# Layer 0 of a two-layer mixture-of-experts trunk: all rows normalised on TensorE and stored plainly, and expert 0's rows made by one-hot products ahead of the overflow branch

## The chip, the core and the metric

One core of a Trainium2 chip runs the whole program. The metric is the device time of one execution in microseconds; the profile's span, which begins with the first recorded instruction, lies within it. Engines: TensorE (PE, with its weight loads as PEld), VectorE (DVE), ScalarE (ACT), GpSimd (POOL), and SyncE (SP), which issues most transfers.

## What is computed

A two-layer backbone over 256 latent and 256 context tokens of width 1024. Each layer has a mixer and then a mixture of 16 experts, of which each token takes two. In layer 0 latent and context tokens go through the experts together, 512 rows in all; in layer 1 only the 256 latent ones. The part that matters here, cut down:

```python
h = rms_norm(x, norm2_g[l]) * (1 + m[:, :, 4]) + m[:, :, 3]
hc = rms_norm(xc, norm2_g[l]) * (1 + mc[:, :, 4]) + mc[:, :, 3]
tokens = jnp.concatenate([h.reshape(-1, D), hc.reshape(-1, D)], axis=0)
...
e_logits = e_logits[jnp.arange(T), g_sel]
top_v, top_i = lax.top_k(e_logits, MOE_TOP_K)
gate = jnp.einsum('tk,tke->te', top_w, jax.nn.one_hot(expert_id, MOE_EXPERTS, dtype=F32))
for e in range(MOE_EXPERTS):
    hid = jax.nn.silu(t @ w1[e]) * (t @ w3[e])
    out = out + gate[:, e:e + 1] * (hid @ w2[e])
```

## The kernel before

The work is written in Python and put in order, engine by engine, by a scheduler; only where a block is wrapped in `in_order(PE)` does TensorE follow the written order. A branch (`tc.If`) ends what can be moved: what is written before it is issued before it or, if the scheduler puts it there, in the block after it. Memory on chip comes from arenas with hand-written `get` and `free`, and a stream of weight pieces of 1 MB each (`self.ws`) fills whatever blocks are given to it, through SyncE's queue (L161). Each piece is split for three-pass products into a rounded part (ScalarE, L339) and a remainder (VectorE or GpSimd, L342), and each product is three matmuls (L348 to L350).

The stages around the change, all in layer 0:

- `finish` ends the mixer. It leaves `H`, the scaled but not yet normalised rows of the latent tokens (`H[0]`) and of the context tokens (`H[1]`), four tiles of 128 rows and 1024 columns, and the router's logits. Ahead of that it fills the two context tiles of the HBM tensor `hd` with the shift row by broadcast (L1339).
- `moe` takes the rows' factors (`rs`), and brings `H` to normalised rows in `hd`. For the two latent tiles TensorE multiplies by a diagonal matrix of the factors (L1440) and adds the shift as a product with three bf16 rows (L1441); ScalarE copies the result over `H[0]` (L1442), and SyncE stores it (L1443). For the two context tiles ScalarE scales in place (L1436), and GpSimd's queue adds the tile to what lies in `hd` (L1437). Meanwhile VectorE picks groups and experts, TensorE counts each row's place within its expert (the rank matmuls, L1486 to L1489), and VectorE makes the ranks (L1501), the gates and the largest count, `mxi` (L1514).
- `experts_rows` has, for each expert, `rows(e)`: a one-hot of its ranks (L1526), eight small matmuls for row numbers and gates (L1562, L1564), the row numbers (L1567), and a gather of up to 128 rows from `hd` through GpSimd's queue (L1530). `take(e)` transposes the gathered rows (L1576), and casts and splits them (L1585, L1586). `first` and `second` are the expert's weight products, the first in two halves of 24 matmuls. The written order is `rows(0)`, `rows(1)`, the overflow branch, and then in TensorE's order `take(0)`, and for each expert e the first half of `first(e)`, `hidden(e - 1)`, `take(e + 1)`, `rows(e + 2)`, the second half, and `second(e - 1)`.
- `overflow` loads `mxi` into a register of every engine (L1857) and branches on it (L1863). Its body, for experts with more than 128 rows, is not entered in this execution.

Of the kernel before, what the change touches and what calls it, by code (L numbers as in the profile page):

```python
# [10 lines left out]
BF = mybir.dt.bfloat16  # L11
I32 = mybir.dt.int32
AF = mybir.ActivationFunctionType
OP = mybir.AluOpType
# [4 lines left out]
P = 128  # L19
D = 1024  # L20
# [232 lines left out]
class Trunk:  # L253
# [1052 lines left out]
    def finish(self, l, mix):  # L1306

        F, nc = self.F, self.nc
        ns = len(self.X)
        A2 = F.get(ns, D)  # L1310
        for s in range(ns):
            self.mod_row(A2[:, s], l, 4, s)

        rts, bR = F.get(ns, KC, 32), F.get(ns, 32)
        self.bR = bR
        for s in range(ns):
            nc.vector.tensor_tensor(rts[:, s], self.rt,
                                    self.a2[l][:, s].rearrange("p (k o) -> p k o", o=1).to_broadcast([P, KC, 32]), op=OP.mult)

        pr, pq = F.get(ns, KC, 32), F.get(ns, 32)  # L1320
        for s in range(ns):
            nc.gpsimd.tensor_tensor(pr[:, s], self.rt,
                                    self.sh[l][:, s].rearrange("p (k o) -> p k o", o=1).to_broadcast([P, KC, 32]), op=OP.mult)
            nc.vector.tensor_reduce(pq[:, s], pr[:, s].rearrange("p k c -> p c k"), AX.X, OP.add)
        ps = self.bank()
        nc.tensor.matmul(ps[:, 0:32 * ns], self.msk("ones"), pq.rearrange("p s c -> p (s c)"), start=True, stop=True)
        nc.scalar.copy(bR, ps[:, 0:32 * ns].rearrange("p (s c) -> p s c", s=ns))
        F.free(pr, pq)
        self.ss, junk = F.get(4, 2), F.get(512, dt=BF)

        H = [F.get(2, D) for s in range(ns)]
        if ns == 2:
            self.hd = self.dp.tile([4 * P, D], F32, name=f"hd{l}")

            self.S3 = F.get(D, dt=BF)
            nc.scalar.dma_start(self.S3[0:3], self.mb2[0].rearrange("i h c -> i (h c)"))
            src = self.md[l, 1][1, :, 1].rearrange("(o h) c -> o h c", o=1)
            for t in range(2, 4):
                nc.scalar.dma_start(self.hd[t * P:(t + 1) * P, :].rearrange("p (h c) -> p h c", h=2),  # L1339
                                    src.to_broadcast([P, 2, 512]))  # L1340
        self.ws.add(F.fits(2048) - FA[l])

        lg, hfR = [self.bank("m"), self.bank("a")][0:ns], Ring(F, 2, 2, 256)
        wait = [], [], []

        def scaled(c, s):
            sl = slice(256 * c, 256 * c + 256)
            nc.vector.tensor_tensor(H[s][:, :, sl], self.X[s][:, :, sl],
                                    A2[:, s, sl].rearrange("p (o c) -> p o c", o=1).to_broadcast([P, 2, 256]), op=OP.mult)

        def logits(c, s):

            ps, hf = self.bank(), hfR()
            for kk in range(2):
                for i in range(2):
                    nc.tensor.transpose(ps[:, 256 * kk + i * P:256 * kk + (i + 1) * P],
                                        self.X[s][:, i, 256 * c + kk * P:256 * c + (kk + 1) * P], self.ident)
            nc.scalar.copy(hf, ps.rearrange("p (k t) -> p k t", k=2))
            for kk in range(2):
                k = 2 * c + kk  # L1360
                j = k % 4
                nc.tensor.matmul(lg[s][32 * j:32 * j + 32, 0:256], rts[:, s, k], hf[:, kk], start=(k < 4), stop=(k >= 4))

        def squares(c, s):
            if c % 2:
                for i in range(2):
                    t = 2 * s + i
                    nc.scalar.activation(junk, self.X[s][:, i, 256 * c - 256:256 * c + 256], AF.Square,
                                         accum_out=self.ss[:, t, c // 2:c // 2 + 1])

        def last(c, s):
            for i, f in enumerate((scaled, squares, logits)):
                wait[i].append((c, s))
                if len(wait[i]) > LAG[i] * ns:
                    f(*wait[i].pop(0))

        self.pool_share = 0
        run_all(self.out_half(l, 1, mix, ns, last))
        for i, f in enumerate((scaled, squares, logits)):
            for cs in wait[i]:  # L1380
                f(*cs)
        F.free(*self.gates, junk, hfR, rts, self.rt, A2)
        self.R.free(*mix)
        if ns == 2:
            self.xgR = Ring(F, 3, D)
            for x in self.xgR.bufs:
                nc.gpsimd.memset(x, 0.0)
        self.ws.add(max(0, F.fits(2048) - FB[l]))
        if l:
            self.swap()  # L1390
        for t in range(2 * ns):
            self.dbg(f"xm{l}_{t}", self.x(t))
        self.moe(l, H, lg)
# [17 lines left out]
    def moe(self, l, hd, lg):  # L1411

        nc, F = self.nc, self.F
# [13 lines left out]
            stt(L[:, t], lp[:, 32 * t:32 * t + 32], rs[:, t:t + 1], self.bR[:, t // 2], op0=OP.mult, op1=OP.add)  # L1427
        if ns == 2:


            H, hd, dgR = hd, self.hd, F.get(2, P)
            for t in range(2):
                nc.scalar.activation(dgR[:, t], self.ident, AF.Copy, scale=rs[:, t:t + 1])
            for t in range(2):
                h, g = H[0][:, t], H[1][:, t]
                nc.scalar.activation(g, g, AF.Copy, scale=rs[:, 2 + t:3 + t])  # L1436
                nc.gpsimd.dma_start(hd[(2 + t) * P:(3 + t) * P, :], g, accum_op=OP.add)  # L1437
                for c in range(2):
                    sl, ps = slice(512 * c, 512 * c + 512), self.bank("a")
                    nc.tensor.matmul(ps, dgR[:, t], h[:, sl], start=True, stop=False)  # L1440
                    nc.tensor.matmul(ps, self.oneb[0:3], self.S3[0:3, sl], start=False, stop=True)  # L1441
                    nc.scalar.copy(h[:, sl], ps)  # L1442
                nc.sync.dma_start(hd[t * P:(t + 1) * P, :], h)  # L1443
            F.free(*H, self.S3, dgR)
        tmp = []

        def T(n):
# [91 lines left out]
    def experts_rows(self, l, nt, hd, rk, G, VAL, mxi):  # L1539
# [16 lines left out]
        def rows(e):  # L1556

            oh = ohR()
            self.one_hot(oh, "iota", rk, e)
            tb = self.bank("m")  # L1560
            for t in range(nt):
                nc.tensor.matmul(tb[:, 0:2], oh[:, t], self.vi[:, t], start=(t == 0), stop=(t == nt - 1))  # L1562
            for t in range(nt):
                nc.tensor.matmul(tb[:, 2:5], oh[:, t], VAL[:, t, e], start=(t == 0), stop=(t == nt - 1))  # L1564
            ohs[e] = oh
            gt, dst, xg = gtR(), ddR(), xgR()
            nc.vector.tensor_scalar(dst, tb[:, 0:1], tb[:, 1:2], BIG, op0=OP.add, op1=OP.add)  # L1567
            self.gather(hd, xg, dst)
            nc.vector.tensor_reduce(gt, tb[:, 2:5], AX.X, OP.add)  # L1569
            st[e] = xg, gt, dst  # L1570

# [7 lines left out]
        def take(e):  # L1579

            xh, xl = xs[e] = xhR(), xlR()
            for b in range(2):
                ps = turn(b, st[e][0])
                pv = ps.rearrange("p (k t) -> p k t", k=4)
                nc.scalar.copy(xh[:, 4 * b:4 * b + 4], pv)  # L1585
                nc.vector.tensor_tensor(xl[:, 4 * b:4 * b + 4], pv, xh[:, 4 * b:4 * b + 4].bitcast(F32),  # L1586
                                        op=OP.subtract)

        def first(e):

# [72 lines left out]
        yy = {}  # L1663
        rows(0)
        rows(1)
        self.overflow(l, nt, P, (rk, G), mxi, xt, put, uR.bufs[0], yR.bufs[0])
        self.ws.add(F.fits(2048))
        self.ws.keep(2, self.end[l])
        with self.in_order(PE):
            take(0)  # L1670
            for e in range(NE + 1):
                f = first(e) if e < NE else iter(())
                next(f, None)
                if e == NE - NP:
                    self.pool_share = 0

                if e:
                    hidden(e - 1)
                if e + 1 < NE:
                    take(e + 1)  # L1680
                if e + 2 < NE:
                    rows(e + 2)
                next(f, None)
                if e:
                    second(e - 1)
                if e == NE - NP:
                    F.free(yR)
                    G2 = [F.get(D) for s in range(2)]
                    for s in range(2):
                        self.mod_row(G2[s], l, 5, s)  # L1690
                    for t in range(nt):
                        back(t, xgR.bufs[1 + t] if t < 2 else None)
        self.pool_share = 2
        F.free(ohR, gtR, ddR, uR)
        if self.early:
# [378 lines left out]
```

## Time and profile before

| what | value |
|---|---|
| three runs | 1195.66, 1200.86, 1201.46 us; median 1200.86 |
| profiled execution | 1201.99 us |
| its span | 1200.2 us |
| TensorE busy | 1084.5 us (90%) |
| VectorE busy | 785.6 us (65%) |
| ScalarE busy | 523.2 us (44%) |
| GpSimd busy | 363.4 us (30%) |
| mean granted clock of TensorE | 0.969 of full |

The span is one execution, in microseconds from its first instruction. Busy is time in which an engine had an instruction running; matmuls overlap their neighbours, so a busy TensorE need not be at its peak. The granted clock is the share of 2.4 GHz that TensorE was given. A wait names the engine or queue whose event came last.

### The profile page before, as it was taken

The numbers are of one execution on the slowest core, as the hardware profiler recorded it, in microseconds if no ns is written. First come the engines' busy times: TensorE is split into PE (matmuls) and PEld (weight loads), VectorE is DVE, ScalarE is ACT, GpSimd is POOL, SyncE is SP. The second block draws the span as 40 slices with busy tenths as digits, with TensorE's granted clock in tenths as the row PEclk, the third lists the DMA queues.
The fourth block names the chain that finished last, engine by engine and source line by source line (L and its number), as shares of the span: only waits on it lengthen the run. The fifth ranks groups of instructions, "written<-read, shape, count | busy, mean of one in ns | idle before, by whom it ended". The sixth has DMA issues, their size and how long they took to land. (4 is left out here: it accounts for less than half of the span.)

```text
span 1200.2 us, 17256 instructions
## 1 busy us (share of the span) xinstructions
PE 1084.5 (90%) x6474; PEld 763.5 (64%) x6474; DVE 785.6 (65%) x1373; ACT 523.2 (44%) x803; POOL 363.4 (30%) x227
## 2 busy tenths in 40 slices
PE   3999978999959999999999897988999879999985
PEld 1666655566827777777788555655677756566552
DVE  2577746756557999999999767699658853222111
ACT  2356534533336888888888432433244310000000
POOL 1332313233212545444451222144342501111111
PEclk9999989999988999999999998999999989999999
DMA  9674477376455999999997615331257799999995
GB/s 352 228 222 130 136 215 236 119 246 241 160 182 212 330 354 365 355 368 378 359 380 250 245 56 194 123 141 71 77 186 288 306 406 409 411 421 413 411 415 203
DMA packets 76321, 317.81 MB, mean 265 GB/s; under 512 B 21269, under 2 KB 27533, under 8 KB 47430
## 3 DMA queue, kind: packets, MB, share of 16 engines
q1 hardware_dynamic: 54656, 294.63, 64.0%
q0 software_dynamic: 6912, 11.25, 4.2%
q10 hardware_dynamic: 14662, 10.73, 3.1%
q8 instruction: 55, 0.90, 0.3%
q14 instruction: 36, 0.29, 0.1%
HBM read 309.43 MB, written 17.92 MB: 273 GB/s over the span
## 5 line engine op out<-in xcount | busy, mean ns | idle before, releaser
L339 ACT CAST arena_rw<-arena_f 128x1024 fp32r<-128x1024 f32 x256 | 266.1, 1049 | 171.9 <-PE b L350 96.3
L342 DVE TENSOR_TENSOR arena_rw<-arena_f,arena_rw 128x1024 fp32r<-128x1024 f32 x198 | 258.5, 1346 | 64.6 <-ACT arena_rw L339 64.3
L348 PE MATMUL b<-arena_rw,arena_rr 128*128 128x512 f32 (+1 forms) x736 | 276.2, 376 | 2.6 <-ACT arena_rr L1610 1.1
L349 PE MATMUL b<-arena_rw,arena_rr 128*128 128x512 f32 (+1 forms) x736 | 274.1, 373 | 0.7 <-DVE arena_rw L342 0.5
L350 PE MATMUL b<-arena_rw,arena_rr 128*128 128x512 f32 (+1 forms) x736 | 269.8, 369 | 1.3 <-DVE arena_rr L1265 1.2
L342 POOL TENSOR_TENSOR arena_rw<-arena_f,arena_rw 128x1024 fp32r<-128x1024 f32 x58 | 155.7, 2685 | 227.3 <-ACT arena_rw L339 201.0
L348 PEld LDWEIGHTS b<-arena_rw,arena_rr 128*128 128x128 f32 x736 | 139.5, 190 | 37.7 <-issue 7.8
L349 PEld LDWEIGHTS b<-arena_rw,arena_rr 128*128 128x128 f32 x736 | 139.4, 189 | 36.7 <-DVE arena_rw L342 10.7
L350 PEld LDWEIGHTS b<-arena_rw,arena_rr 128*128 128x128 f32 x736 | 138.6, 189 | 27.3 <-issue 1.9
L1780 ACT ACTIVATE arena_f<-b 128x256 f32<-128x256 f32 x16 | 6.1, 384 | 194.5 <-PE b L1773 194.5
L1535 POOL DMA_INDIRECT out<-arena_f x16 | 24.9, 1555 | 211.3 <-DVE arena_f L1806 207.3
L1773 PE MATMUL b<-arena_f 128*64 128x256 f32 x672 | 77.9, 381 | 4.1 <-DMA arena_f<-in_moe 4.0
L437 PE MATMUL b<-arena_f,cs 128*32 128x256 f32 x768 | 67.9, 416 | 14.8 <-DMA arena_f<-in_modw 14.6
L348 PE MATMUL b<-arena_rr,arena_rw 128*128 128x512 f32 (+1 forms) x192 | 73.8, 389 | 3.2 <-ACT arena_f L912 1.7
L350 PE MATMUL b<-arena_rr,arena_rw 128*128 128x512 f32 (+1 forms) x192 | 72.7, 382 | 4.5 <-DVE arena_rw L342 4.5
L349 PE MATMUL b<-arena_rr,arena_rw 128*128 128x512 f32 (+1 forms) x192 | 72.2, 377 | 1.4 <-POOL arena_rr L537 1.4
L1773 PEld LDWEIGHTS b<-arena_f 128*64 128x64 f32 x672 | 47.8, 137 | 31.9 <-issue 6.8
L437 PEld LDWEIGHTS b<-arena_f,cs 128*32 128x32 f32 x768 | 21.2, 112 | 48.4 <-issue 29.5
L348 PEld LDWEIGHTS b<-arena_rr,arena_rw 128*128 128x128 f32 x192 | 36.5, 191 | 17.2 <-issue 5.8
L1806 DVE SCALAR_TENSOR_TENSOR arena_f<-b,arena_f 128x512 f32<-128x512 f32 x16 | 12.0, 751 | 54.0 <-PE b L1801 54.0
L584 POOL TENSOR_TENSOR arena_f<-arena_f 128x512 f32<-128x512 f32 x21 | 29.6, 1415 | 55.2 <-DVE arena_f L581 53.1
L1530 POOL DMA_INDIRECT arena_f<-hd,arena_f x16 | 27.4, 1713 | 60.4 <-DVE arena_f L1569 50.4
(380 smaller groups left out, 1688.1 us busy)
## 6 DMA issues: line engine op xcount, KB each, us to landing
arena_f<-in_moe SPq DMA_DIRECT2D x192, 1024.0 KB
arena_f<-in_modw SPq DMA_DIRECT2D x96, 512.0 KB
arena_f<-in_wod SPq DMA_DIRECT2D x18, 1024.0 KB
arena_f<-in_wev SPq DMA_DIRECT2D x14, 1024.0 KB
arena_f<-md ACTq DMA_DIRECT2D x8, 512.0 KB
arena_f<-in_tok SPq DMA_DIRECT2D x4, 512.0 KB
yd<-arena_f SPq DMA_DIRECT2D x4, 512.0 KB
arena_f<-yd SPq DMA_DIRECT2D x4, 512.0 KB
```

Of the source, the lines that this page charges most:

```text
L339: nc.scalar.copy(h, raw)
L342: eng.tensor_tensor(l, raw, h.bitcast(F32), op=OP.subtract)
L348: nc.tensor.matmul(ps, ah, bh, start=first, stop=False)
L349: nc.tensor.matmul(ps, ah, bl, start=False, stop=False)
L350: nc.tensor.matmul(ps, al, bh, start=False, stop=last)
L437: nc.tensor.matmul(acc[32 * i:32 * i + 32, 0:256], self.cs[:, k, :], raw[:, i * 256:(i + 1) * 256], start=(k == 0), stop=(k == KC - 1))
L584: (nc.vector if last and c == 3 else nc.gpsimd).tensor_tensor(xs, xs, tmp, op=OP.add)
L1530: self.nc.gpsimd.indirect_dma_start(out=xg, out_offset=None, in_=hd[:, :], in_offset=bass.IndirectOffsetOnAxis(ap=tk, axis=0), bounds_chec ...
L1535: self.nc.gpsimd.indirect_dma_start(out=yd[:, :], out_offset=bass.IndirectOffsetOnAxis(ap=dst, axis=0), in_=y, in_offset=None, bounds_chec ...
L1773: nc.tensor.matmul(p[64 * c:64 * c + 64, 0:256], x[:, 4 * b + k], raw[:, 512 * k + 256 * c:512 * k + 256 * c + 256], start=(b == 0 and k = ...
L1780: nc.scalar.activation(u, ps[0], AF.Tanh, scale=0.5)
L1806: nc.vector.scalar_tensor_tensor(y, py, gt, G2, op0=OP.mult, op1=OP.mult)
```

## The change

All four tiles of rows are multiplied by a diagonal matrix on TensorE, get their shift there, are copied over `H` and stored by SyncE with plain transfers; the broadcasts into `hd` ahead of them, the scaling on ScalarE and the two accumulating transfers of GpSimd's queue go. `H` stays on chip longer. Expert 0 has no gather: its one-hot is copied to f32, and its rows, already transposed, are 32 f32 products of `H` with the one-hot. `take(0)` is written ahead of the overflow branch. The ring of gather buffers starts at expert 1, so the buffers that are used again at the end have other numbers.

```diff
-            self.S3 = F.get(D, dt=BF)
-            nc.scalar.dma_start(self.S3[0:3], self.mb2[0].rearrange("i h c -> i (h c)"))
-            src = self.md[l, 1][1, :, 1].rearrange("(o h) c -> o h c", o=1)
-            for t in range(2, 4):
-                nc.scalar.dma_start(self.hd[t * P:(t + 1) * P, :].rearrange("p (h c) -> p h c", h=2),
-                                    src.to_broadcast([P, 2, 512]))
+            self.S3 = F.get(2, D, dt=BF)
+            for s in range(2):
+                nc.scalar.dma_start(self.S3[0:3, s], self.mb2[s].rearrange("i h c -> i (h c)"))
...
-            for t in range(2):
-                h, g = H[0][:, t], H[1][:, t]
-                nc.scalar.activation(g, g, AF.Copy, scale=rs[:, 2 + t:3 + t])
-                nc.gpsimd.dma_start(hd[(2 + t) * P:(3 + t) * P, :], g, accum_op=OP.add)
+            for t in range(nt):
+                h = H[t // 2][:, t % 2]
                 for c in range(2):
                     sl, ps = slice(512 * c, 512 * c + 512), self.bank("a")
                     nc.tensor.matmul(ps, dgR[:, t], h[:, sl], start=True, stop=False)
-                    nc.tensor.matmul(ps, self.oneb[0:3], self.S3[0:3, sl], start=False, stop=True)
+                    nc.tensor.matmul(ps, self.oneb[0:3], self.S3[0:3, t // 2, sl], start=False, stop=True)
                     nc.scalar.copy(h[:, sl], ps)
                 nc.sync.dma_start(hd[t * P:(t + 1) * P, :], h)
-            F.free(*H, self.S3, dgR)
+            self.H = H
+            F.free(self.S3, dgR)
...
-            self.gather(hd, xg, dst)
+            if e:
+                self.gather(hd, xg, dst)
...
+            if e == 0:
+                ohf = F.get(nt, P)
+                nc.scalar.copy(ohf, ohs[0])
             for b in range(2):
-                ps = turn(b, st[e][0])
+                if e:
+                    ps = turn(b, st[e][0])
+                else:
+                    ps = self.bank()
+                    for k in range(4):
+                        for t in range(nt):
+                            nc.tensor.matmul(ps[:, k * P:(k + 1) * P],
+                                             self.H[t // 2][:, t % 2, (4 * b + k) * P:(4 * b + k + 1) * P], ohf[:, t],
+                                             start=(t == 0), stop=(t == nt - 1))
...
+            if e == 0:
+                F.free(ohf, *self.H)
...
         rows(0)
         rows(1)
+        take(0)
         self.overflow(l, nt, P, (rk, G), mxi, xt, put, uR.bufs[0], yR.bufs[0])
...
-            take(0)
```

On TensorE, the last instructions ahead of the overflow branch. Before (the rows of the small matmuls of expert 0 end there; `b_` names are banks for results):

```order
L1564 LDWEIGHTS arena_f
L1564 MATMUL b_2629<-arena_f 128x3
L1857 TENSOR_LOAD arena_f
L1863 COMPARE_AND_BRANCH
L1867 COMPARE_AND_BRANCH
```

and behind the branch, before:

```order
L1863 UNCONDITIONAL_BRANCH
L1562 LDWEIGHTS arena_f
L1562 MATMUL b_2644<-vi,arena_f 128x2
...
L1576 MATMUL b_2962<-mskt,arena_f 128x128 x4
L1576 MATMUL b_2969<-mskt,arena_f 128x128 x4
L348 MATMUL b_2976<-arena_rw,arena_rr 128x512
```

Of the change, both sides of the branch (lines are those of the new program: L1588 is the one-hot product, L1557 and L1559 the small matmuls):

```order
L1559 MATMUL b_2643<-arena_f 128x3
L1588 MATMUL b_2670<-arena_f 128x128 x2
L1557 LDWEIGHTS arena_f
L1557 MATMUL b_2655<-vi,arena_f 128x2
...
L1588 MATMUL b_2670<-arena_f 128x128 x14
L1588 MATMUL b_2689<-arena_f 128x128 x16
L1866 TENSOR_LOAD arena_f
L1872 COMPARE_AND_BRANCH
...
L1872 UNCONDITIONAL_BRANCH
L348 MATMUL b_3014<-arena_rw,arena_rr 128x512
```

The 32 products and the small matmuls of expert 1 moved ahead of the branch, the transposes of expert 0 are gone, and the weight products follow the branch directly.

On GpSimd's queue at the same place, before:

```order
L1387 MEMSET arena_f 128x1024
L1437 DMA hd_2205<-arena_f 128x1024 x2
L1857 TENSOR_LOAD arena_f
L1863 COMPARE_AND_BRANCH
...
L1863 UNCONDITIONAL_BRANCH
L1530 DMA arena_f<-hd_2205,arena_f 128x1024 x2
```

and in the change:

```order
L1384 MEMSET arena_f 128x1024 x2
L1525 DMA arena_f<-hd_2205,arena_f 128x1024
L1866 TENSOR_LOAD arena_f
L1872 COMPARE_AND_BRANCH
...
L1872 UNCONDITIONAL_BRANCH
L342 TENSOR_TENSOR arena_rw<-arena_f,arena_rw 128x1024
```

The two accumulating stores are gone, and the gather of expert 1 (L1530 before, L1525 now) is issued ahead of the branch.

On SyncE's queue, where layer 1 begins, behind the last weights of layer 0 (`in_wod` are mixer weights, `in_modw` modulation weights). Before:

```order
L161 DMA arena_f<-in_wsm 128x256
L161 DMA arena_f<-in_wod 128x2048
L161 DMA arena_f<-in_modw 128x1024 x8
L161 DMA arena_f<-in_wod 128x2048
L428 DMA arena_f<-in_modb 32x256 x6
```

and in the change:

```order
L161 DMA arena_f<-in_wsm 128x256
L161 DMA arena_f<-in_modw 128x1024
L161 DMA arena_f<-in_wod 128x2048
L161 DMA arena_f<-in_modw 128x1024 x7
L161 DMA arena_f<-in_wod 128x2048
L428 DMA arena_f<-in_modb 32x256 x8
```

One transfer of modulation weights now stands ahead of the first mixer weights.

## Rows read from the trace of the kernel before

**Rows 1.** Windows: stretch, then busy us and count per engine, granted clock, DMA share, GB/s.

```profile
300.00:400.00 100.00, 79.92 (x479) 61.75 (x480) 62.56 (x118) 48.12 (x75) 26.23 (x17) 0.88 0.56 196
520.00:540.00 20.00, 19.99 (x98) 15.63 (x97) 19.14 (x20) 16.59 (x20) 9.43 (x4) 1.00 1.00 366
1000.00:1100.00 100.00, 100.00 (x810) 62.36 (x808) 26.56 (x72) 6.03 (x16) 12.47 (x8) 1.00 1.02 413
```

**Rows 2.** Waits in 400 to 640 us: who waited for whom, total us, times, longest.

```profile
ACT arena_rw L339 <- PE b L350: 29.4, 78, 0.6
```

**Rows 3.** Waits in 340 to 370 us.

```profile
POOL arena_f L1530 <- SPq L1863: 9.5, 1, 9.5
PE b L1576 <- DMA arena_f<-hd,arena_f: 8.7, 1, 8.7
PE b L1562 <- PEq L1863: 5.2, 1, 5.2
```

**Rows 4.** Timeline to 354 us: start, us, engine, line, operation; idle before and releaser.

```profile
339.44 1.12 PE L1440 MATMUL b<-arena_f 128*128 128x512 f32 x2 [0.82 <-ACT arena_f L1433]
344.94 0.18 PE L1487 MATMUL b<-arena_f,bfs 128*128 128x16 bf16 x1
345.04 0.59 ACT L1442 COPY arena_f<-b 128x512 f32<-128x512 f32 x1 [0.68 <-PE b L1441]
345.49 0.22 DVE L1501 SCALAR_TENSOR_TENSOR arena_f<-b,arena_f 128x64 f32<-128x64 f32 x1
345.99 0.68 DVE L1526 TENSOR_TENSOR arena_f<-mskt,arena_f 128x512 bf16<-128x512 f32 x1
348.17 0.25 PE L1564 MATMUL b<-arena_f 128*128 128x3 bf16 x4 [1.19 <-DVE arena_f L1508]
353.30 1.11 POOL L1530 DMA_INDIRECT arena_f<-hd,arena_f  x1 [9.52 <-SPq L1863]
353.61 0.19 PEld L1562 LDWEIGHTS <-arena_f 128*128 128x128 bf16 x4 [5.28 <-issue]
```

**Rows 5.** Timeline of TensorE, 362 to 373 us.

```profile
362.72 1.94 PE L1576 MATMUL b<-mskt,arena_f 128*128 128x128 f32 x8 [8.74 <-DMA arena_f<-hd,arena_f]
364.48 0.79 PE L348 MATMUL b<-arena_rw,arena_rr 128*128 128x512 f32 x1
368.49 0.49 PE L348 MATMUL b<-arena_rw,arena_rr 128*128 128x512 f32 x1
372.08 1.04 PE L1576 MATMUL b<-mskt,arena_f 128*128 128x128 f32 x8
```

**Rows 6.** Groups by line and form from 660 us (busy us, mean ns), and the timeline.

```profile
L1758 PE MATMUL b<-arena_f 128*128 128x128 f32 x256 | 32.0, 286 | 1.3 <-DVE arena_f L1508 1.3
...
972.08 5.88 PE L1758 MATMUL b<-arena_f 128*128 128x128 f32 x32 [1.33 <-DVE arena_f L1508]
```

**Rows 7.** Lines L1857 and L1863, load and branch: ns min/median/max, first and last start.

```profile
L1857 PEldq TENSOR_LOAD <-arena_f x2: 579/841/1103, 348.3 to 1189.3; - x2
...
L1863 PEldq COMPARE_BRANCH  x2: 3321/3636/3952, 349.5 to 1189.9; - x2
L1863 DVEq COMPARE_BRANCH  x2: 63/68/72, 349.8 to 1191.6; - x2
```

**Rows 8.** Windows of 1 us (columns as in rows 1).

```profile
347.00:348.00 1.00, 0.00 (x0) 0.00 (x0) 0.93 (x4) 0.00 (x0) 0.00 (x0) 1.00 1.03 205
348.00:349.00 1.00, 0.25 (x4) 0.16 (x3) 0.66 (x4) 0.00 (x0) 0.00 (x0) 0.60 1.15 229
368.00:369.00 1.00, 1.00 (x4) 0.79 (x3) 0.48 (x1) 0.49 (x1) 0.00 (x0) 0.66 0.08 16
```

**Rows 9.** The tensor hd: its gathers from issue to landing.

```profile
DMA to landing us min/median/max: 5.5/9.3/10.4
```

**Rows 10.** Waits of TensorE, 640 to 1000 us.

```profile
PE b L906 <- DVE arena_f L897: 6.7, 3, 4.5
PE b L350 <- DVE arena_rw L342: 4.5, 1, 4.5
```

More of the change, by code (lines that the diff above doesn't have):

```diff
@@ L1428, in moe @@
         if ns == 2:
-            H, hd, dgR = hd, self.hd, F.get(2, P)
-            for t in range(2):
+            H, hd, dgR = hd, self.hd, F.get(nt, P)
+            for t in range(nt):
                 nc.scalar.activation(dgR[:, t], self.ident, AF.Copy, scale=rs[:, t:t + 1])
-            for t in range(2):
-                h, g = H[0][:, t], H[1][:, t]
-                nc.scalar.activation(g, g, AF.Copy, scale=rs[:, 2 + t:3 + t])
-                nc.gpsimd.dma_start(hd[(2 + t) * P:(3 + t) * P, :], g, accum_op=OP.add)
+            for t in range(nt):
+                h = H[t // 2][:, t % 2]
                 for c in range(2):
@@ L1565, in rows @@
             ohs[e] = oh
-            gt, dst, xg = gtR(), ddR(), xgR()
+            gt, dst, xg = gtR(), ddR(), xgR() if e else None
             nc.vector.tensor_scalar(dst, tb[:, 0:1], tb[:, 1:2], BIG, op0=OP.add, op1=OP.add)
-            self.gather(hd, xg, dst)
+            if e:
+                self.gather(hd, xg, dst)
             nc.vector.tensor_reduce(gt, tb[:, 2:5], AX.X, OP.add)
@@ L1581, in take @@
             xh, xl = xs[e] = xhR(), xlR()
+            if e == 0:
+                ohf = F.get(nt, P)
+                nc.scalar.copy(ohf, ohs[0])
             for b in range(2):
-                ps = turn(b, st[e][0])
+                if e:
[3 more added lines that the diff above has]
+                    for k in range(4):
+                        for t in range(nt):
+                            nc.tensor.matmul(ps[:, k * P:(k + 1) * P],
+                                             self.H[t // 2][:, t % 2, (4 * b + k) * P:(4 * b + k + 1) * P], ohf[:, t],
+                                             start=(t == 0), stop=(t == nt - 1))
                 pv = ps.rearrange("p (k t) -> p k t", k=4)
@@ L1691, in experts_rows @@
                     for t in range(nt):
-                        back(t, xgR.bufs[1 + t] if t < 2 else None)
+                        back(t, xgR.bufs[t] if t < 2 else None)
         self.pool_share = 2
```

## The prediction

> **What bounds the kernel now.** I read the busy time by stretch first. In the stretch of the first layer's experts TensorE has no idle time and the clock is full, while the DMA engines are busy too [rows 1]; ScalarE's splits of the weights wait there for TensorE to give their buffers back, never for a transfer [rows 2]. So TensorE bounds that stage, and a later start of it is a later end. In the second layer's experts the DMA engines are the full ones [rows 1], but their queue of weights is released by the stages before, so a shift ahead of it moves it as a whole. The stretch that the change touches lies between 339 and 372 us, and the list of waits says what ends last there: TensorE waits 5.2 us for its own branch and then 8.7 us for the first gather [rows 3]. The timeline gives the steps: diagonal products from 339.44, the rank matmuls at 344.94, the last small matmul before the branch at 348.17, back from the branch at 353.61 [rows 4], the transposes of the first gathered rows at 362.72, the first weight matmul at 364.48 and the second expert's transposes at 372.08 [rows 5]. The last of these is my mark: in both programs the 24 matmuls of the first half of expert 0 stand directly ahead of it.
>
> **The change part by part**, against the profiled execution (1201.99 us, of which the span is 1200.2; the median of the three runs is 1.13 us lower, at 1200.86).
>
> (a) *Four more diagonal products in front of the ranks.* The old four take (344.94 - 339.44) / 4 = 1.375 us each [rows 4]; TensorE goes from one to the next, and the copies of 0.59 us keep up. All eight stand ahead of the rank matmuls in the new order, so these begin 4 x 1.375 = 5.50 us later, at 350.44. What goes for it, two scalings on ScalarE, two accumulating transfers on GpSimd's queue and two broadcasts to HBM some 150 us earlier, is on engines for which nobody on this path waits: nothing. It was covered by TensorE's products, and still would be.
>
> (b) *From the ranks to the first one-hot product.* VectorE makes the ranks 0.55 us after the rank matmuls begin, and the one-hot of expert 0 is done 1.73 us after (345.99 + 0.68 - 344.94) [rows 4]. Three small operations now stand ahead of the ranks instead of between, so I take 1.6. Then ScalarE copies the one-hot to f32: no row shows that, the nearest is its copy of the same size at 0.59 [rows 4], with a hand-over 0.7. The first product starts at 350.44 + 2.3 = 352.75.
>
> (c) *The one-hot products.* The second layer does the same with f32 products of the same shape. There 128 products are 256 instructions and 32.0 us [rows 6], so one product is two instructions of 0.125 us, and the 32 of the change take 64 x 0.125 = 8.0 us at the full clock. The small matmuls of expert 1, which the order puts in between, add two groups of 0.25 [rows 4]. End: 361.25. The upper bound is the halved clock: the first 32 of the second layer took 5.88 us instead of 4.0 because they began at it [rows 6], and eight transposes of the first take need 1.94 us where later ones need 1.04 [rows 5], thus 0.243 for one instruction and 15.5 us for all. I take the full clock, and say why under the first rival.
>
> (d) *The branch, now behind the products.* TensorE's load of the count takes 1.10 us here and 0.58 in the second layer, its compare and branch 3.95 and 3.32 [rows 7]; with 0.15 for the hand-over 5.2 at this place, 4.05 by the lower values. I take 5.2, because it is the same branch: 366.45. The other engines branch in well under 0.1 us [rows 7], and their last work, the cast and the difference of the second half, ends before 363. The Trainium skill (Advanced Engine Details and Errata, Control Flow Timing) gives about 108 ns for a compare and branch. By that figure the step would be 1.1 + 0.1 + 0.15 = 1.35 us and the sum 3.85 us lower; this trace shows 3.95 and 3.32 on TensorE, and the rows decide.
>
> (e) *Expert 0 starts without gather or transposes.* The 8.7 us of waiting and the 1.76 us from the transposes to the first weight matmul (364.48 - 362.72) are gone [rows 3, 5]. Before, the clock was halved until inside 368 to 369 [rows 8], and the 24 matmuls took 7.60 us. After 5.2 us without work I expect the same: 366.45 + 7.60 = 374.05, against 372.08. Bounds: the 15 matmuls from 368.49 on take 3.59 us, 0.239 each, so all 24 at the full clock 5.7, which is 1.9 less; the nine before that take 4.01, 0.446 each, so all 24 at half 10.7, which is 3.1 more.
>
> (f) *The gather of expert 1* is issued ahead of the branch now, behind all four plain stores. The last store leaves at about 351; should it take 5.5 us, like the shortest gather, and the gather the 9.3 of the median [rows 9], the rows are there at 366, eight before they are wanted. Nothing. SyncE's next weights wait for the same stores, so they start later, but eight weight transfers stand ahead of the branch in both orders, more than expert 0 opens with: nothing. One more weight buffer (10 for 9) feeds a stage that TensorE bounds: nothing.
>
> (g) *The rest of the program in another order.* Memory blocks move, and the scheduler orders the second layer's mixer differently: one weight transfer stands behind a modulation transfer, and VectorE makes several small constants earlier. I cannot price that from the order. Two of TensorE's longest waits in that stretch are 4.5 us each [rows 10], both on VectorE: to win or lose one of them is the bound, 4.5 either way, and I take nothing.
>
> Sum: 374.05 - 372.08 = **+2.0 us**; 1204.0 for a profiled execution, 1202.9 on the median.
>
> **Rivals.** First, **slower: the clock falls before the products**. Before the change it fell inside 348 to 349 [rows 8], three us after the rank matmuls, with only small matmuls between. Now the first product starts some two us after the ranks, and eight diagonal products run ahead of them instead of four, which speaks against it; but in between TensorE has only eight small matmuls. It decides if the clock is down when the first product starts and stays down: 7.5 us more, 1210.4. The Trainium skill (TensorE: Matmul & The Clock Gate, What's actually happening) has the halved clock as the default that activity releases; by that rule this gap is the place where it could return, and the rows of the old gap agree.
> Second, **faster: the new order of the second layer frees TensorE** of both waits of 4.5 us on VectorE: 1202.9 - 9.0 = 1193.9. For it: the small constants that stood on VectorE before these waits now stand earlier. Against: a scheduler has no reason to hit both.
> Third, **the branch costs TensorE next to nothing** behind busy work: 3.85 less, 1199.1. Both rows of (d) speak against it. It is what the Trainium skill's page named under (d) would have.
> Fourth, **the gather wait comes back one expert later**, so that the change only moves it: the stores would have to land eight us later than in (f); each us beyond is one lost, 1207 with four.
> Fifth, **the new order costs one wait** of 4.5 us more: 1207.4.
>
> **How the numbers follow.** A measurement of this kernel tells about 0.5%, 6 us, from no change (the three runs lie 5.8 us apart), so the bounds are 1194.9 and 1206.9. Chances: the forecast 0.57, the third rival 0.03, both within the bounds: 0.60. Faster, the second rival: 0.16. Slower: 0.14 for the clock, 0.05 for each of the last two, 0.24. The range reaches down to the forecast less the lower values of (d) and (e) and one wait of (g), 1202.9 - 1.15 - 1.9 - 4.5 = 1195, and up to the clock's price, 1210.
>
> **What would show it.** Right: rank matmuls near 350.4; 64 instructions of one-hot products in about 8 us; TensorE back from the branch 5.2 us after the last of them; no wait for a gather in the first two experts; the second expert's transposes near 374. Wrong: products at 0.24 us each; a branch on TensorE of under one us; a wait on the gather at expert 1; a distance from there to the end other than before by more than 4.5 us.

## The result and the profile after

| kernel | median of its runs, us | ratio to the kernel before, 95% interval |
|---|---|---|
| changed kernel, 20 runs | 1206.47 | 1.0051 [1.0033, 1.0069] |
| the same once more, 12 runs (a2_after) | 1204.83 | 1.0025 [0.9996, 1.0054] |

The change makes the kernel slower by 0.25 to 0.5%, 3 to 6 us, on the border of what can be told from no change: the first interval is clear of 1, the second is not. The forecast was 2.0 us slower, and 1206.47 lies within its range. The sum came out a few us low, and by terms that were off in both directions, as the profile shows. The profiled execution of the changed kernel took 1204.28 us, with a span of 1202.5. The page's first part:

```profile
PE 1100.8 (92%) x6542; PEld 773.7 (64%) x6542; DVE 783.4 (65%) x1373; ACT 524.8 (44%) x808; POOL 361.3 (30%) x224
```

TensorE is busy 16 us more than before (1084.5), and the median grows by a third of that: much of the new work stands where it waited. The timeline of TensorE in the stretch that the change touches (start, us, operation; idle before and releaser), to set against [rows 4, 5]:

```profile
338.06 1.89 PE L1434 MATMUL b<-arena_f 128*128 128x512 f32 x2 [0.82 <-ACT arena_f L1429]
340.42 1.74 PE L1434 MATMUL b<-arena_f 128*128 128x512 f32 x2
342.41 1.12 PE L1434 MATMUL b<-arena_f 128*128 128x512 f32 x2
...
350.65 0.18 PE L1482 MATMUL b<-arena_f,bfs 128*128 128x16 bf16 x1
...
352.90 0.71 PE L1588 MATMUL b<-arena_f 128*128 128x128 f32 x4 [0.35 <-ACT arena_f L1580]
...
353.66 6.94 PE L1588 MATMUL b<-arena_f 128*128 128x128 f32 x60
363.17 0.47 PE L348 MATMUL b<-arena_rw,arena_rr 128*128 128x512 f32 x1 [2.57 <-PEq L1872]
...
368.85 1.03 PE L1572 MATMUL b<-mskt,arena_f 128*128 128x128 f32 x8
```

The products end at 360.60. The wait for the branch is 2.57 us, not 5.2; the 24 matmuls of the first half take 5.68 (363.17 to 368.85), not 7.60; and the mark, the second expert's transposes, is at 368.85, where 374.05 was forecast. The list of TensorE's waits in this stretch (330 to 380 us: in total, times, longest) has no gather in it:

```profile
PE b L348 <- PEq L1872: 2.6, 1, 2.6
PE b L1557 <- DVE arena_f L1509: 1.0, 1, 1.0
PE b L1434 <- ACT arena_f L1429: 0.8, 1, 0.8
PE b L1588 <- ACT arena_f L1580: 0.3, 1, 0.3
```

So this execution was 3.2 us ahead of the one before at the mark (372.08) and 2.3 behind at the end; 1.4 of the 3.2 lie ahead of the first diagonal product (338.06 for 339.44), in work that the change leaves alone. The windows (columns as in rows 1) show the other side of step (a): the first two diagonal pairs (a product with the diagonal matrix and the one for its shift) ran for the most part at the halved clock.

```profile
338.00:340.00 2.00, 1.94 (x3) 0.42 (x3) 1.83 (x14) 1.10 (x5) 0.00 (x0) 0.57 0.00 0
340.00:342.00 2.00, 2.00 (x3) 0.50 (x2) 1.76 (x10) 0.59 (x1) 0.00 (x0) 0.58 0.00 0
342.00:344.00 2.00, 2.00 (x6) 0.70 (x6) 0.44 (x2) 0.70 (x2) 0.00 (x0) 1.00 0.04 14
```

### The profile page after: what moved, and what is told of

It is laid out like the page before. It is cut to its first block, busy times and chain, and to the rows that moved or that the text cites. A ratio compares the mean times of both kernels' runs of the same rounds, so it can differ in the third digit from the quotient of the medians.

```text
span 1202.5 us, 17391 instructions
## 1 busy us (share of the span) xinstructions
PE 1100.8 (92%) x6542; PEld 773.7 (64%) x6542; DVE 783.4 (65%) x1373; ACT 524.8 (44%) x808; POOL 361.3 (30%) x224
## 5 line engine op out<-in xcount | busy, mean ns | idle before, releaser
L342 POOL TENSOR_TENSOR arena_rw<-arena_f,arena_rw 128x1024 fp32r<-128x1024 f32 x58 | 155.4, 2680 | 226.2 <-ACT arena_rw L339 199.1
L1530 POOL DMA_INDIRECT out<-arena_f x16 | 24.9, 1559 | 209.0 <-DVE arena_f L1815 205.2
L1782 PEld LDWEIGHTS b<-arena_f 128*64 128x64 f32 x672 | 47.7, 137 | 30.8 <-issue 6.0
L1525 POOL DMA_INDIRECT arena_f<-hd,arena_f x15 | 26.6, 1770 | 68.2 <-DVE arena_f L1565 50.4
```

What stands on the lines that cost most here:

```text
L342: eng.tensor_tensor(l, raw, h.bitcast(F32), op=OP.subtract)
L1525: self.nc.gpsimd.indirect_dma_start(out=xg, out_offset=None, in_=hd[:, :], in_offset=bass.IndirectOffsetOnAxis(ap=tk, axis=0), bounds_chec ...
L1530: self.nc.gpsimd.indirect_dma_start(out=yd[:, :], out_offset=bass.IndirectOffsetOnAxis(ap=dst, axis=0), in_=y, in_offset=None, bounds_chec ...
L1782: nc.tensor.matmul(p[64 * c:64 * c + 64, 0:256], x[:, 4 * b + k], raw[:, 512 * k + 256 * c:512 * k + 256 * c + 256], start=(b == 0 and k = ...
```

## The experiments

Theory 1, from these two profiles: the lead at the mark is real, and the new order of layer 1 loses it. The first four kernels were made to test that.

### The memory alone, with the order it brings: e1_layout

```diff
-            self.S3 = F.get(D, dt=BF)
+            S3_ = F.get(2, D, dt=BF)
+            self.S3, self.S3_ = S3_[:, 0], S3_
...
-            H, hd, dgR = hd, self.hd, F.get(2, P)
+            H, hd, dgR = hd, self.hd, F.get(nt, P)
...
-            F.free(*H, self.S3, dgR)
+            self.H = H
+            F.free(self.S3_, dgR)
...
+        xgR.i = -1
         rows(0)
         rows(1)
+        ohf = F.get(nt, P)
+        F.free(ohf, *self.H)
...
```

> The kernel before, with its own work in layer 0 (gather, accumulating transfers), but with the memory of the changed kernel: the same blocks are taken and given back at the same places of the program. The order of layer 1's mixer then comes out as in the changed kernel on TensorE, VectorE, GpSimd and ScalarE. Theory 1 (the order of layer 1, which the memory layout alone decides, costs the time: the changed kernel is 3.2 us ahead at the second expert's transposes and 5.7 us behind at the end): about 8.9 us over the kernel before, 1209.6, and at least 1206. Rival (the loss comes from what layer 0 does differently, and the order costs nothing): 1200.7, as before.

Measured: 1199.58 us, 0.9998 [0.9974, 1.0023]. The 8.9 us of theory 1 are not there: in the whole time memory and order cost nothing that can be told. But the memory changes layer 0 as well. SyncE's weights start later (355.00), and the small matmuls of expert 1 stand ahead of the branch, so that one wait holds the branch and the gather (waits of TensorE, 337 to 380 us):

```profile
PE b L1578 <- DMA arena_f<-hd,arena_f: 4.6, 1, 4.6
```

The kernel before waits 5.2 and 8.7 there [rows 3]. In the profile of e1_layout the mark comes 27.9 us behind the first diagonal product (32.6 before), and from the mark to the end it takes 832.8 us (828.1 before). So the whole time may be a gain in layer 0 and a loss in layer 1, and this run alone does not clear the memory of a price in layer 1.

### The order pinned: e5_pin

```diff
+        by = {i.name: i for i in self.nc.cur_bb.bb.instructions}
+        for seq in json.loads(zlib.decompress(base64.b85decode(ORDER))).values():
+            prev = None
+            for r in seq:
+                i = by.get(f"I-{base + r}")
...
+                if prev is not None:
+                    self.tc.add_manual_dep(i, prev.name, NOSYNC, reason="pin")
+                prev = i
```

> The changed kernel, with the order of every engine in layer 1 (from the end of layer 0's experts to the second overflow branch) pinned to that of the kernel before. Theory 1: the 3.2 us gained at the second expert's transposes stay to the end, 1197.5. Rival (the loss is not in the order): 1206.5, as the changed kernel. A third outcome, about 1200.7, would say that the transfers of layer 1 swallow the lead of layer 0.

Measured: 1206.02, 1.0050 [1.0026, 1.0075], as the changed kernel. So the order is not what costs the time; the memory of the changed kernel is still in it. Its diagonal products and its ranks took from 339.54 to 355.24, with the clock at half for ten of these 16 us:

```profile
340.00:344.00 4.00, 4.00 (x7) 0.82 (x5) 3.54 (x21) 1.19 (x5) 0.00 (x0) 0.54 0.00 0
344.00:350.00 6.00, 6.00 (x8) 1.57 (x8) 2.33 (x13) 1.84 (x4) 0.00 (x0) 0.50 0.22 87
350.00:352.00 2.00, 2.00 (x5) 0.39 (x3) 0.00 (x0) 0.59 (x1) 0.00 (x0) 0.86 0.65 262
```

### The stores alone: e2_stores

```diff
-            gt, dst, xg = gtR(), ddR(), xgR() if e else None
+            gt, dst, xg = gtR(), ddR(), xgR()
...
-            if e:
-                self.gather(hd, xg, dst)
+            self.gather(hd, xg, dst)
...
-        take(0)
...
         self.overflow(l, nt, P, (rk, G), mxi, xt, put, uR.bufs[0], yR.bufs[0])
...
         with self.in_order(PE):
+            take(0)
```

> One part of the change alone: all four tiles through TensorE and stored plainly, but expert 0 gathered and transposed as before, behind the branch. Layer 1 has the order of the changed kernel. Theory 1: the ranks come 5.5 us later than before, the gather is issued at about 355 and lands at about 365.5, so the second expert's transposes are at about 375, 2.8 later than before, and with the order's 8.9 the time is 1212. If the order costs nothing: 1203.5. If the stores hold the gather back more than that, TensorE waits for it for longer than 6 us after its branch.

Measured: 1207.43, 1.0046 [1.0021, 1.0070]. Memory and layer 1's order are those of e1_layout, so the 0.48% between the two, 5.8 us, is what eight diagonal pairs and four plain stores cost in place of the old way; the two intervals touch, but e11_layout_pin below (at most 1.0012) is clear of this one. That it is about step (a)'s 5.5 is no proof of that step: the profile has the mark 29.0 us behind the first diagonal product, where those of e1_layout and e11_layout_pin have 27.9 and 25.9. The mark was not at 375: the gather took 3.9 us from its issue and no 9.3, so the transposes were at 366.62. The changed kernel (1.0051 and 1.0025) is not to be told from this one: the one-hot products are worth about what the gather was.

### The ranks ahead of the last diagonal products: e4_ranks_first

The loop of the diagonal products moves from ahead of the routing to this place:

```diff
         rp = self.bank()
...
+        if ns == 2:
+            for t in range(nt):
+                h = H[t // 2][:, t % 2]
...
+            F.free(self.S3, dgR)
         red(gw, ge, AX.X, OP.add)
```

> The changed kernel with the rank products written ahead of the diagonal products, so that TensorE has them behind the fifth of eight and the chain ranks, one-hot, f32 copy runs on VectorE and ScalarE beside the last three. Layer 1 is in the same order as in the changed kernel on every engine. If layer 0's lead goes through to the end, the 2.25 us between the ranks' start and the first one-hot product (350.65 to 352.90) shrink to under 0.3: 2.0 us less, 1204.5. If the second layer's transfers set the end whatever comes before: 1206.5.

Measured: 1203.75, 1.0032 [1.0012, 1.0052], 2.7 under the changed kernel's 1206.47. In its profile the first one-hot product follows the last diagonal pair at once (354.47 and 355.00, with small matmuls in between), as intended. What layer 0 saves there does seem to reach the end, but the intervals overlap.

### Both kernels once more: a2_after and b2_before

> The changed kernel once more, for a second profile beside that of the kernel before on the same chip. Theory 2 (the first four profiles of kernels with eight diagonal products show the clock at half for 3 to 10 us from their start on, in each to another extent): 1206.5 again, the rank products between 350.6 and 356, and the second expert's transposes between 368.9 and 375, in step with them. If the first profile is typical in all, the transposes are at 368.9 within 0.5.

> The kernel before once more, for a second profile. In the first the gather of expert 0 was issued 0.4 us behind SyncE's first weights and took 9.4 us; in e1_layout, whose weight buffers come free later, it was issued 3.9 us ahead of them and took some 4.6. If the buffers decide: SyncE's weights start before the gather again, and the second expert's transposes are near 372. If it is chance: the transposes may be anywhere from 365 on.

a2_after stands in the table above. Its profile has the mark at 378.46: ranks at 356.32, products from 358.58 to 369.05, 10.5 us, and 7.23 for the 24 matmuls. b2_before took 1195.05 in its one run. In it SyncE's weights started ahead of the gather again (351.70 and 352.35), and the gather was there all the same after 5.2 us, as the waits of TensorE show (337 to 367 us):

```profile
PE b L1562 <- PEq L1863: 4.3, 1, 4.3
PE b L1576 <- DMA arena_f<-hd,arena_f: 2.2, 1, 2.2
```

So the 8.7 us of [rows 3] are no constant: 2.2 here, 8.5 in e10_fill_before. Which of the two starts first does not settle it. The number of weight transfers (1 MB each) near the gather fits all six profiles with a gather of expert 0: with two of them issued within 0.7 us of it, the transposes began 9.4 and 9.3 us behind its issue (before, e10_fill_before); with one so near and the next 2.6 us later (354.94), 5.2 (here); with none ahead, 4.7, 4.2 and 3.9 (e1_layout, e11_layout_pin, e2_stores). No run varied this alone, so it is not shown to be the cause.

### The idle time ahead of the diagonal products filled: e8_fill, e10_fill_before

```diff
+        if ns == 2:
+            fl = self.bank("a")
+            for _ in range(2):
+                nc.tensor.matmul(fl[:, 0:256], lgs[:, 1, 0:P], lgs[:, 1], start=True, stop=True)
         for t in range(nt):
             stt(L[:, t], lp[:, 32 * t:32 * t + 32], rs[:, t:t + 1], self.bR[:, t // 2], op0=OP.mult, op1=OP.add)
```

> The changed kernel with two products more, whose result nobody reads, on TensorE between the router's last transposes and the first diagonal product, where it sat idle for 0.82 us. Every other instruction has its place. Theory 2: the idle stretch is what lets the clock fall at the diagonal products; filled, the eight take 11.0 us (1.375 each) in place of the 12.6, 12.6 and 15.7 of the three profiles with all eight in a row, and the time is about 3 us less than the changed kernel's, 1203.5. Rival (the thin work ahead, from 334 on, does it): the clock falls as before and the time is 1206.5.

> The kernel before with the same two idle products at the same place. Theory 2: it has four diagonal products at risk and not eight, so it gains at most half of what the changed kernel gains, 1 to 1.5 us: 1199.5. Rival: no change, 1200.7.

e8_fill: 1203.08, 1.0014 [0.9985, 1.0043]; e10_fill_before: 1202.91, 1.0004 [0.9980, 1.0028]. In both profiles the clock stayed full through the diagonal products. That is little evidence for theory 2: of the twelve profiles with the idle time, three (before, e11_layout_pin, e12_onehot) have the clock full there as well. e8_fill:

```profile
343.82 1.12 PE L1438 MATMUL b<-arena_f 128*128 128x512 f32 x2
...
354.80 0.18 PE L1486 MATMUL b<-arena_f,bfs 128*128 128x16 bf16 x1
...
368.70 0.47 PE L348 MATMUL b<-arena_rw,arena_rr 128*128 128x512 f32 x1 [2.32 <-PEq L1876]
```

Eight pairs take 354.80 - 343.82 = 10.98 us, 1.37 each, which is step (a)'s price to the hundredth. The time goes the way theory 2 says for the changed kernel, by an amount that its interval does not secure; the kernel before gains nothing.

### The two other pairs on the order, and the products behind the branch: e11_layout_pin, e6_ranks_pin, e3_take_behind

The first two have the pin of e5_pin on e1_layout and on e4_ranks_first; the third has this edit:

```diff
         rows(1)
-        take(0)
+        ohf0 = F.get(nt, P)
+        F.free(*self.H)
         self.overflow(l, nt, P, (rk, G), mxi, xt, put, uR.bufs[0], yR.bufs[0])
-        self.ws.add(F.fits(2048))
...
         with self.in_order(PE):
+            take(0)
+            self.ws.add(F.fits(2048))
```

> The kernel e1_layout (work of before, memory of the changed kernel) with the order of layer 1 pinned to that of the kernel before: the layout of layer 0 without its effect on the order. From the second expert's transposes to the end of the span four profiles with the order of before took 828.1, 826.9, 831.1 and 828.3 us, six with the changed order 832.8, 834.8, 833.7, 829.8, 832.5 and 828.2, 3.4 more in the mean, while the whole times of e1_layout and e5_pin showed no such price. Theory 3 (the order costs these 3.4, and in e1_layout the later weights gave them back at the gather): 3.4 less than e1_layout, 1196.5 beside 1200.7, and 828.5 behind the transposes. Rival (chance of the clock in single executions): as e1_layout, 1200.

> e4_ranks_first with the order of layer 1 pinned to that of the kernel before: the second such pair. Theory 3: 3.4 less than e4_ranks_first's 1203.8, 1200.4, as fast as the kernel before. Rival: 1203.8.

> The changed kernel with expert 0's one-hot products behind the overflow branch on TensorE, and the gather of expert 1 behind it on GpSimd; the last weight buffers come free after the products. Were the branch entered, its body would overwrite rows that the products still read; it is not entered here. If TensorE's queue runs ahead of the engine, so that products in front of the branch cover a part of it: here only small matmuls stand in front, TensorE waits the whole 4.3 to 5.3 us for the branch in place of the 2.2 to 2.6 of the five profiles, the clock is at half when the products begin, and they take 10 to 12 us in place of 7.7 to 10.5: 4 us more than the changed kernel, 1209.5. Rival (the branch is short because TensorE is warm, wherever it stands): no change, 1205.5.

e11_layout_pin: 1199.96, 0.9997 [0.9982, 1.0012], as without the pin, and 834.9 us from the second expert's transposes to the end, not 828.5: theory 3 falls too. e6_ranks_pin: 1203.27, 1.0011 [0.9994, 1.0028] beside 1.0032, not clear of it. Of three pairs none shows a price of the order. e3_take_behind: 1209.83, 1.0071 [1.0043, 1.0099], as forecast. Its timeline:

```profile
358.86 0.24 PE L1559 MATMUL b<-arena_f 128*128 128x3 bf16 x4
363.16 9.59 PE L1588 MATMUL b<-arena_f 128*128 128x128 f32 x64 [4.06 <-PEq L1874]
372.51 0.47 PE L348 MATMUL b<-arena_rw,arena_rr 128*128 128x512 f32 x1
```

With only small matmuls in front, the branch makes TensorE wait 4.06 us; the products took 9.6 us, a little under the forecast of 10 to 12.

### The one-hot products alone: e12_onehot

```diff
+            for t in range(2):
+                h, g = H[0][:, t], H[1][:, t]
+                nc.scalar.activation(g, g, AF.Copy, scale=rs[:, 2 + t:3 + t])
+                nc.gpsimd.dma_start(hd[(2 + t) * P:(3 + t) * P, :], g, accum_op=OP.add)
...
+                for t in range(2, nt):
+                    nc.tensor.matmul(pi[0:3, 0:P], self.oneb[:, 0:3], ohs[0][:, t], start=(t == 2), stop=(t == nt - 1))
+                nc.vector.tensor_copy(ind[0:3], pi[0:3, 0:P])
...
+                        nc.tensor.matmul(ps[:, k * P:(k + 1) * P], self.S3[1][0:3, (4 * b + k) * P:(4 * b + k + 1) * P],
+                                         ind[0:3], start=False, stop=True)
```

> The other part of the change alone: the stores of before (two latent tiles through TensorE, two context tiles scaled on ScalarE and added by GpSimd's queue to the shift that lies in memory), and expert 0's rows by f32 one-hot products ahead of the branch. The context rows lie on chip without their shift, so each of the eight groups of products gets one bf16 product more, of the three shift rows with a row that says which places hold a context row. If the four more diagonal pairs are what the changed kernel pays (e2_stores beside e1_layout: 5.8 us) and the products with the shorter branch are worth the gather: 5.5 to 6 us less than the changed kernel's two medians (1206.5, 1204.8), 1200, with 5.5 for the diagonal products, 8.5 for the one-hot products, 2.2 to 2.6 of waiting for the branch, and the second expert's transposes some 25 us behind the first diagonal product, where the kernel before has 27.9 to 32.6. If that lead over the kernel before reaches the end as well: 1196. Rival (the products and their hand-overs cost more than the gather): 1203 or more.

Measured: 1213.25, 1.0125 [1.0082, 1.0169], the slowest of all. Windows and timeline of its profile:

```profile
344.00:346.00 2.00, 0.62 (x13) 0.33 (x9) 1.96 (x10) 0.93 (x2) 0.00 (x0) 1.00 1.05 328
346.00:350.00 4.00, 3.90 (x19) 3.49 (x20) 1.60 (x8) 0.05 (x1) 0.00 (x0) 0.50 0.94 252
350.00:354.00 4.00, 4.00 (x24) 3.27 (x22) 1.01 (x4) 0.00 (x0) 1.12 (x1) 0.50 0.09 17
354.00:358.00 4.00, 4.00 (x19) 3.32 (x17) 0.69 (x1) 0.59 (x1) 0.00 (x0) 0.50 0.04 14
```

```profile
346.10 2.07 PE L1599 MATMUL b<-arena_f 128*128 128x128 f32 x8 [0.19 <-ACT arena_f L1587]
...
359.95 1.16 PE L1599 MATMUL b<-arena_f 128*128 128x128 f32 x8
...
361.20 1.16 PE L1599 MATMUL b<-arena_f 128*128 128x128 f32 x8
...
364.62 0.48 PE L348 MATMUL b<-arena_rw,arena_rr 128*128 128x512 f32 x1 [2.10 <-DVEq L1885]
```

This is the first rival of the prediction, in another kernel: behind four diagonal pairs the clock was at half when the products began, and they took 16.3 us (346.10 to 362.36), with the eight bf16 products and small matmuls between them. At the full clock a group of eight f32 instructions and its bf16 product takes 1.25 us here (359.95 to 361.20), so about 10 us for all would be an estimate without the fall. That eats the 5.5 us of four pairs less: the mark comes 32.1 us behind the first diagonal product, within the 27.9 to 32.6 of the kernel before. The loss came in layer 1, whose order differs once more in this kernel: its mixer takes 323.7 us, where the kernel before has 307 to 311. So the run does not tell what the one-hot products alone are worth. Two waits of TensorE there, where the changed kernel's longest at the same places are 1.7 and 0.2 us (in total, times, longest):

```profile
PE b L1363 <- ACT arena_f L1359: 4.7, 3, 3.8
PE b L452 <- DVE arena_f L444: 4.5, 1, 4.5
```

So a new order can cost a wait of 4.5 us, as the fifth rival said; in the changed kernel it did not.

## Why the prediction was right, and where its steps were not

The profiles, cut at four events: the first diagonal product, the mark, the end of layer 0's experts (the first weight matmul behind the last wait for `hidden`), layer 1's rank matmuls and the end of the span. From the mark to the end of layer 0's experts all take 290.8 to 290.9, so TensorE bounds that stage, as read in [rows 1, 2]. The others, in us (e5_pin, e6_ranks_pin and e11_layout_pin have the old order of layer 1, all rows but the first the new memory):

| kernels | first diagonal product to mark | layer 1's mixer, to its ranks | ranks to end |
|---|---|---|---|
| before, b2_before, e10_fill_before | 32.6, 27.9, 31.7 | 307.5, 306.9, 311.0 | 229.7, 229.1, 229.2 |
| after, a2_after, e8_fill, e5_pin | 30.8, 34.7, 30.6, 35.2 | 316.6, 312.3, 315.9, 311.4 | 226.1, 226.6, 225.8, 226.2 |
| e4_ranks_first, e6_ranks_pin | 31.8, 30.3 | 310.4, 316.0 | 227.1, 226.2 |
| e1_layout, e11_layout_pin | 27.9, 25.9 | 315.5, 317.3 | 226.6, 226.7 |

The forecast, 34.6 in the first column for 32.6 before, lies among the changed kernel's values; the means of the three plain profiles (after, a2_after, e5_pin: 33.6) and of the two plain ones before (30.3) differ by 3.3 where it said 2.0, and by 2.1 with the filled kernels (e8_fill, e10_fill_before) taken in on both sides. That is luck in part:

- **(a)** was right at the full clock (10.98 for eight pairs in e8_fill). In the three plain profiles the clock fell as they began, and ranks came 12.6, 12.6 and 15.7 us after the first product. The price of the halved clock was left out of this step. The kernel before can meet it too: its four pairs took 5.5 us in the execution shown and 8.7 in b2_before (338.54 to 347.23), with the same 0.8 us of idle time ahead of them [rows 4].
- **(b)** was right: 2.25 us from the ranks to the first product, for 2.3.
- **(c)** was right in the first profile: 7.7 us (352.90 to 360.60) for 8.0 and the small matmuls. In a2_after, e5_pin and e8_fill they took 9.2 to 10.5, for the clock was at half for a part of them. In a2_after it fell 0.8 us before they began and in e5_pin 0.1 before, both behind eight pairs; in e8_fill 0.9 after. So the reason that the first rival gave against itself, the eight pairs ahead, did not hold: its fall came in two of these four profiles, but it lasted 6.8 us in a2_after and 3.4 in e5_pin, and the products took 2.8 and 1.5 us more than in the first profile, not 7.5. Timeline and windows of a2_after:

```profile
358.58 1.22 PE L1588 MATMUL b<-arena_f 128*128 128x128 f32 x4 [0.33 <-ACT arena_f L1580]
```

```profile
357.00:360.00 3.00, 1.80 (x21) 1.65 (x22) 2.28 (x8) 0.63 (x2) 0.00 (x0) 0.63 0.43 175
360.00:363.00 3.00, 3.00 (x15) 3.00 (x16) 0.89 (x3) 0.00 (x0) 1.23 (x1) 0.50 0.04 11
```

  The Trainium skill (TensorE: Matmul & The Clock Gate, What's actually happening) has the halved clock as the default that activity releases; these windows agree, with 0.50 behind small matmuls. The first profile, with the same small matmuls and the clock full, shows that it need not fall there.
- **(d)** failed: "I take 5.2, because it is the same branch." The branch is the same, 3.7 us, but it no longer starts behind TensorE's last work. Lines L1866 and L1872 of the changed kernel:

```profile
L1866 PEldq TENSOR_LOAD <-arena_f x2: 487/541/595, 358.6 to 1192.0; - x2
...
L1872 PEldq COMPARE_BRANCH  x2: 3339/3524/3708, 359.1 to 1192.7; - x2
```

  The load starts at 358.6, 2.0 us ahead of the last product's end: TensorE's queue runs ahead of its engine. It did so by 2.0 us in all six profiles of kernels with the change's products in front, and the wait was 2.2 to 2.6 there, and 4.1 with them behind (e3_take_behind). The third rival was right in direction and too bold in size. By the 108 ns of the Trainium skill (Advanced Engine Details and Errata, Control Flow Timing) there would have been no wait left at all, as an estimate; the shortest branch of TensorE in any profile here takes 3.30 us (a2_after).
- **(e)** took the wrong one of its three values: behind a gap of 2.6 us the clock was full and the 24 matmuls took 5.68, the lower bound, and so in e5_pin, e8_fill and e4_ranks_first. In a2_after it fell 0.2 us after they began, and they took 7.23. Together (d) and (e) were 3 to 5 us too high.
- **The mark before** was the other error. I took one execution's gather wait, 8.7 us, as the kernel's. In b2_before it was 2.2, in e10_fill_before 8.5. Branch and gather together held TensorE up for 13.9 us in the execution shown, 6.5 and 13.8 in these two, and 4.6 and 7.7 with the new memory (e1_layout, e11_layout_pin): the execution shown had the longest. What the change removes was therefore worth less than the sum had it.
- **(f)** held: no wait for a gather in the changed kernel's first experts.
- **(g)**, taken as nothing, held for the order: three pairs with and without the pin show no price. But with the new memory layer 1's mixer took 310 to 317 us in ten profiles (315.0 and 317.4 in e3_take_behind and e2_stores), where the old memory has 307 to 311 in three, with nearly the same waits when the order is pinned; the clock was at half for 27 to 46 us of it in the ten, and for 21.5, 21.5 and 29.3 in the three. Layer 1's experts give 3 us back, and so do not move as a whole, as I had it: TensorE waits 8.0 us for their weights before and 4.5 in the changed kernel, presumably since they had more time to arrive. Both together make layer 1 longer by 3.4 us in the mean of the ten, which (g) does not have; the single profiles overlap (537.5 to 544.0 for 535.9 to 540.2). Whole runs with the new memory and the old work show no price (e1_layout 0.9998, e11_layout_pin 0.9997), but their layer 0 is shorter (first column of the table). Whether the clock falls more often there for a reason or by chance stays open.

What can be called shown, from whole times with the same memory: the stores' part costs the time (e2_stores 1.0021 to 1.0070, where the old stores have 0.9974 to 1.0023 and 0.9982 to 1.0012), the one-hot part beside it gives or takes nothing that can be told, the order nothing. Where in the program the 5.8 us of the stores lie is not shown: the profile of e2_stores has 1.2 and 3.1 us of them at the mark. That diagonal pairs at the half clock make a part of it is argued from the profiles and e8_fill, whose own interval is too wide to prove it. Less clock over the whole execution is not the cause: the mean granted clock was 0.968 in both sets of the changed kernel (20 and 12 runs) and 0.965 to 0.967 in four sets of the kernel before (11 to 33 runs). A mean does not tell whether TensorE had work while it was at half, though. And a price of the new memory in layer 1, hidden in e1_layout by its shorter layer 0, is a rival that no run tells apart. None of the versions is faster than the kernel before.

## What to carry to other kernels

Price a removed wait by several executions: a wait on a transfer that was 8.7 us in one profile was 2.2 in the next. A branch costs an engine less than its row says if the engine's queue still holds work when it reaches it, so put long products, not short ones, ahead of it; here TensorE then waited 2.2 to 2.6 us in place of 4.1. Read the granted clock of added work in several executions: the same products cost 7.7 us at the full clock and 10.5 where it was at half for a part of them. And a kernel that is no slower as a whole, like e1_layout, may still pay in one stage what it gains in another: compare by stages before a theory is dropped.

## What was not expected

At 205 us, in work that is the same in all kernels, the clock falls in all fourteen profiles; in a2_after it stays down for 14 us longer (to 228) than in the changed kernel's first profile (to 215). Windows of that one and, below, of a2_after:

```profile
205.00:215.00 10.00, 8.20 (x33) 3.59 (x27) 10.00 (x24) 6.23 (x18) 2.08 (x2) 0.51 0.82 298
215.00:225.00 10.00, 10.00 (x58) 5.73 (x54) 6.43 (x21) 5.38 (x17) 2.47 (x3) 0.98 0.50 170
```

```profile
205.00:215.00 10.00, 8.95 (x33) 3.65 (x32) 10.00 (x24) 6.22 (x18) 2.08 (x2) 0.50 0.81 293
215.00:225.00 10.00, 10.00 (x29) 4.22 (x25) 3.43 (x12) 1.96 (x6) 2.08 (x2) 0.50 0.35 115
225.00:230.00 5.00, 5.00 (x30) 4.24 (x28) 2.67 (x7) 2.51 (x9) 0.00 (x0) 0.69 0.36 111
```

Its first diagonal product is at 343.73 and not at 338.06: 5.7 us lost ahead of the change, as much as the change costs. e8_fill and e3_take_behind begin as late (343.82, 343.74). A single execution of this kernel cannot tell an effect of a few us.
